# Attention value products in blocks of three key tiles, tied in TensorE's issue order, with the row sums at the head of a block

## Chip, cores and metric

The kernel runs on one core of a Trainium2 chip. The metric is the device time of one execution in microseconds; lower is better.

## What is computed

Two layers of a hybrid backbone over 512 latent tokens with 256 context tokens, model width 1024, all in float32. Layer 0 mixes tokens by multi-head latent attention, layer 1 by a Hyena convolution, and each layer has a gated ConvFFN. The change is in the attention of layer 0: 16 heads, 512 queries, 768 keys (256 of context, 512 latent), head width 96 for scores and 64 for values.

```python
def block_attention(q, k, v):
    def one_block(qblk):
        s = jnp.einsum('bqhd,bkhd->bhqk', qblk, k).astype(F32) * scale
        p = jax.nn.softmax(s, axis=-1).astype(v.dtype)
        return jnp.einsum('bhqk,bkhd->bqhd', p, v)
    o = lax.map(one_block, qb)
    return o.transpose(1, 0, 2, 3, 4).reshape(B, Lq, H * v.shape[-1])

x = x + g1 * (ox @ mla_w_o[j])
```

## The kernel before

Weights and activations are split into a high part rounded to the format fp32r and a low remainder, and a product is three matmuls (high x high, high x low, low x high; `mm3`, L136 to L139). Only the value products and the row sums are in plain float32, each one matmul in the program and two on the chip, as the counts in the trace show.

The attention loop (`attention`, L646, its loop at L842) goes over eight pairs of heads p, in a pair over six key tiles kt of 128 keys, in a tile over the two heads b. For each it does:

- `s_step` (L731): three matmuls give the scores of 128 keys by 512 queries in a PSUM tile `s`; ACT's exponential (L740) writes them to `pf`; GpSimd (POOL) adds `pf` to the head's running sum `acc` (L750; DVE in the last two heads' last tiles). The scores' 97th row carries the negative row maximum of each query, so that the exponential stays in range.
- `side` (L818): work for the next pair n = p + 1, one step a call: rope rows by DMA (`put_rope`), the key products `pk` (`prod_k`, L635), the query products `pq` (`prod_q`, L704), the split of the next query weight where n is odd (`load_wq`: ACT cast L129, DVE subtraction L130), then eight `max_step` (L712): two matmuls into a PSUM tile `sm` of one buffer, and DVE's maximum over it (L721, `mx`). `max_row` (L723) turns four such columns into a row by four small matmuls `mr`, and ACT copies it into the queries (L727). At the end of even pairs it makes the rope part of two more pairs (`prod_rope`, L673: products `pq`, rotation `rot`, DVE steps).
- `v_step` (L754): the value products. The two heads of a pair write the two halves of a PSUM tile `po`, 64 columns of the array each: column tiling. A call takes two key tiles, four products, every second tile, one step behind the scores.
- `row_sums` (L768): a matmul of ones (32 columns wide) with `acc` for each head gives the sums, ACT copies 64 rows of them (L775), two DMAs write them to DRAM, one reads them back as 16 x 64 (L779), DVE takes the reciprocal (L780), and two DMAs broadcast it to 128 partitions (`rb`, L784).
- `normalize` (L787): DVE multiplies the pair's output `ou` by `rb`, ACT casts it to `oh`, DVE subtracts for `ol`.

PSUM tiles of `pst` (scores, key and query products, `mr`, row sums, `rot`) share four buffers. The order on each engine's queue is fixed when the program is built: a scheduler takes the instructions, their dependencies and free buffers, and lists them for each engine; at run time each engine goes through its list in order. So the program's order of calls is only a wish, and value products of one call may be issued apart.

Of the kernel before, what the change touches and what calls it, by code (L numbers as in the profile page):

```python
# [8 lines left out]
F32 = mybir.dt.float32  # L9
# [8 lines left out]
P = 128  # L18
D = 1024
NC = D // P  # L20
T = 512
# [36 lines left out]
def hybrid_kernel(ctx, tc, A, out):  # L58
    nc = tc.nc
    dma = nc.sync.dma_start  # L60
# [1 line left out]
    stt = nc.vector.scalar_tensor_tensor  # L62
    vtt = nc.vector.tensor_tensor
    vts = nc.vector.tensor_scalar
    mm = nc.tensor.matmul

    gp = ctx.enter_context(tc.tile_pool(name="gp", bufs=1, side="right"))
    wp = ctx.enter_context(tc.tile_pool(name="wp", bufs=2, side="right"))
# [4 lines left out]
    def in_order(prev, cur):  # L73
        if prev is not None:
            info = mybir.DependencyInfo(mybir.DependencyClass.NoSync, mybir.DependencyReason.DATA)
            tc.add_manual_dep(cur.ins, prev.ins.name, info, reason="issue order")
        return cur

    def pst(name):
        return psum[0].tile([P, 512], F32, tag="ps", name=name, bufs=psum[1])  # L80

    def pso(name):
        return psum[0].tile([P, 512], F32, tag="o", name=name, bufs=2)
# [22 lines left out]
    ones = gp.tile([P, P], F32, name="ones")  # L106
# [125 lines left out]
    class Norm:  # L232
# [18 lines left out]
        def add(self, xj, h=None):  # L251
            self.n_add += 1
            self.flush(self.nh)
            n, w = self.n, self.nth * P
            hs = list(range(self.nh)) if h is None else [h]
            j = self.j[hs[0]]
            for i in hs:
                self.j[i] += 1
            if j == 0 and n > 2:
                self.acc = self.tmp.tile([P, self.nt * P], F32, tag="sqa", name="sqa", bufs=1)  # L260
                act(out=self.acc, in_=xj, func=AF.Square)
                return
            sq = self.tmp.tile([P, self.nt * P], F32, tag="sq", name="sq", bufs=2)[:, :w * len(hs)]
            if j < n - 1 and n > 2:
                act(out=sq, in_=xj, func=AF.Square)  # L265
                acc = self.acc[:, hs[0] * w:hs[-1] * w + w]
                nc.gpsimd.tensor_tensor(out=acc, in0=acc, in1=sq, op=ALU.add)  # L267
                if j == n - 2:
                    for i in hs:
                        self.due.append((self.n_add, self.acc[:, i * w:(i + 1) * w], i, True, False))  # L270
                return
            vtt(out=sq, in0=xj, in1=xj, op=ALU.mult)
            for i, q in enumerate(hs):
                self.due.append((self.n_add, sq[:, i * w:(i + 1) * w], q, j == 0, j == n - 1))
# [191 lines left out]
    rst = [[dr.tile([2, T], F32, name=f"rst{a}{p}") for p in range(HEADS // 2)] for a in range(2)]  # L466

    def mla():
# [56 lines left out]
        with ExitStack() as st:  # L525
            ab = st.enter_context(tc.tile_pool(name="ab", bufs=1, side="left", reuse_waits="tile"))
            psum_pool(st, "pb", 4)
            return attention(ab, L)
# [117 lines left out]
    def attention(ab, L):  # L646
        at, cosq, sinq, cqh, cql = (L[n] for n in ("at", "cos", "sin", "cqh", "cql"))
# [12 lines left out]
        vf = {}  # L660
# [68 lines left out]
        pts, accs = {}, {}  # L729

        def s_step(h, kt):  # L731
            kh, kl = kb[h % 4]
            qh, ql = qb[h % 4]
            ks = slice(kt * P, kt * P + P)
            s = pst("s")
            mm(s, lhsT=kh[0:97, ks], rhs=qh[0:97], start=True, stop=False)
            mm(s, lhsT=kh[0:96, ks], rhs=ql[0:96], start=False, stop=False)
            mm(s, lhsT=kl[0:96, ks], rhs=qh[0:96], start=False, stop=True)  # L738
            pf = ab.tile([P, T], F32, tag="pf", name="pf", bufs=8)
            act(out=pf, in_=s, func=AF.Exp, scale=ATT_SCALE)  # L740
            pts[h, kt] = pf
            if kt == 0:
                return
            if kt == 1:
                accs[h] = ab.tile([P, T], F32, tag="acc", name="acc", bufs=4)
                prev = pts[h, 0]
            else:
                prev = accs[h]
            add = vtt if h >= HEADS - 2 and kt > 3 else nc.gpsimd.tensor_tensor
            add(out=accs[h], in0=prev, in1=pf, op=ALU.add)  # L750

        pos = {}

        def v_step(p, kts):  # L754
            if kts[0] == 0:
                pos[p] = pso("po")
            for kt in kts:
                for b in range(2):
                    mm(pos[p][64 * b:64 * b + 64], lhsT=vf[p][:, kt, b, :], rhs=pts.pop((2 * p + b, kt)),
                       start=kt == 0, stop=kt == 5)  # L760
            if kts[-1] == 5:
                ou = ab.tile([P, T], F32, tag="ou", name="ou", bufs=2)
                nc.scalar.copy(out=ou, in_=pos.pop(p))
                ends.append((p, ou))

        ends, norm = [], []

        def row_sums():  # L768
            while ends:
                p, ou = ends.pop(0)  # L770
                rsum = pst("rsum")
                for b in range(2):
                    mm(rsum[32 * b:32 * b + 32], lhsT=ones[:, 0:32], rhs=accs.pop(2 * p + b), start=True, stop=True)
                sm = at.tile([P, T], F32, tag="wv", name="sm", bufs=4)
                nc.scalar.copy(out=sm[0:64], in_=rsum[0:64])  # L775
                for b in range(2):
                    dma(out=rst[0][p][b:b + 1, :], in_=sm[32 * b:32 * b + 1])
                rs = ab.tile([16, 64], F32, tag="rs", name="rs", bufs=1)
                dma(out=rs, in_=rst[0][p].rearrange("b (a c) -> (b a) c", c=64))  # L779
                nc.vector.reciprocal(out=rs, in_=rs)  # L780
                dma(out=rst[1][p].rearrange("b (a c) -> (b a) c", c=64), in_=rs)
                rb = ab.tile([P, T], F32, tag="rb", name="rb", bufs=1)
                for b in range(2):
                    dma(out=rb[64 * b:64 * b + 64], in_=rst[1][p][b].partition_broadcast(64))  # L784
                norm.append((p, ou, rb))

        def normalize():  # L787
            while norm:
                p, ou, rb = norm.pop(0)
                vtt(out=ou, in0=ou, in1=rb, op=ALU.mult)  # L790
                nc.scalar.copy(out=oh[:, p, :], in_=ou)
                vtt(out=ol[:, p, :], in0=ou, in1=oh[:, p, :], op=ALU.subtract)

        NP = HEADS // 2
# [4 lines left out]
        for h in range(2):  # L799
            m2 = ab.tile([P, 4, 2], F32, tag="m2", name="m2", bufs=2)  # L800
            mxs[h] = ab.tile([P, 4], F32R, tag="mx", name="mx", bufs=2)
            for qt in range(4):
                for i in range(2):
                    b1 = pst("b1")[:, :384]
                    mm(b1, lhsT=qb[h][0][0:96, qt * P:(qt + 1) * P], rhs=kb[h][0][0:96, i * 384:(i + 1) * 384],
                       start=True, stop=True)
# [11 lines left out]
        def side(n, i):  # L818
            if i == 11 and n % 2 and n + 1 < NP:
                prod_rope((n + 1) // 2)  # L820
            if n >= NP:
                return
            if i == 0:
                put_rope(n)
                if n > 1:
                    prod_k(n, 0, kb, L)
            elif i == 1 and n > 1:
                prod_k(n, 1, kb, L)
            elif i == 2:
                if n > 1:  # L830
                    prod_q(n)
                if n % 2 and n // 2 + 1 < 4:
                    load_wq(n // 2 + 1)
            elif 2 < i < 11:
                max_step(2 * n + (i - 3) // 4, (i - 3) % 4)
                if i == 6 or i == 10:
                    max_row(2 * n + (i == 10))
                if i == 9 and n + 1 < NP:
                    load_v(n + 1)

        pend = []
        for p in range(NP):  # L842
            for kt in range(6):
                for b in range(2):
                    s_step(2 * p + b, kt)
                    side(p + 1, 2 * kt + b)
                if kt % 2 == 0 and pend:
                    v_step(*pend.pop(0))
                if kt == 1:
                    row_sums()  # L850
                if kt == 4:
                    normalize()
                if kt % 2:
                    pend.append((p, (kt - 1, kt)))
        v_step(*pend.pop(0))
        row_sums()
        normalize()
        return oh, ol

# [412 lines left out]
```

## Time and profile before

| | us |
|---|---|
| median of 3 runs | 1474.65 |
| lowest, highest | 1473.51, 1474.66 |
| profiled execution, time | 1473.2 |
| profiled execution, span | 1471.4 |

| engine | busy us | share of the span |
|---|---|---|
| PE (TensorE matmuls) | 1412.3 | 96% |
| PEld (weight loads) | 1086.9 | 74% |
| DVE (VectorE) | 952.1 | 65% |
| ACT (ScalarE) | 556.6 | 38% |
| POOL (GpSimd) | 223.6 | 15% |

The span runs from the first to the last instruction; the time also has what lies around it. A busy time is a sum over records, and matmuls overlap at their ends, so the cost of a matmul in a queue is read from its start to the next start. In a row of the timeline the first number is the start, the second the time from the first start to the last end, and the brackets give an idle time ahead of it and what ended it. Names of tiles follow the program: `po<-pf,vf` is a value product, `rsum<-acc,ones` a row sum, `sm<-kh,qh` a row-maximum product, `mx<-sm` its reduction, `s<-...` a score product, `pj<-...` the output projection behind the loop.

### The profile page before, as it was taken

The numbers are of one execution on the slowest core, as the hardware profiler recorded it, in microseconds if no ns is written. First come the engines' busy times: TensorE is split into PE (matmuls) and PEld (weight loads), VectorE is DVE, ScalarE is ACT, GpSimd is POOL, SyncE is SP. The second block draws the span as 40 slices with busy tenths as digits, with TensorE's granted clock in tenths as the row PEclk, the third lists the DMA queues.
The fourth block names the chain that finished last, engine by engine and source line by source line (L and its number), as shares of the span: only waits on it lengthen the run. The fifth ranks groups of instructions, "written<-read, shape, count | busy, mean of one in ns | idle before, by whom it ended". The sixth has DMA issues, their size and how long they took to land. (4 is left out here: it accounts for less than half of the span.)

```text
span 1471.4 us, 17226 instructions
## 1 busy us (share of the span) xinstructions
PE 1412.3 (96%) x6702; PEld 1086.9 (74%) x6702; DVE 952.1 (65%) x1423; ACT 556.6 (38%) x845; POOL 223.6 (15%) x188
## 2 busy tenths in 40 slices
PE   6899899999998999999999999999899999999997
PEld 3577655555478878787887887887798888888886
DVE  5875655555458877657774589889776553355545
ACT  5444444445423543214432352333234432243420
POOL 4401044343511000000000103321310000000011
PEclk9999999999999999999999999999999999999998
DMA  9672411111363564674522352222323213332121
GB/s 376 210 275 90 136 41 47 33 54 44 123 208 122 174 217 149 222 282 158 185 99 102 129 178 94 87 86 87 114 87 115 78 59 107 115 105 87 59 79 58
DMA packets 46668, 186.56 MB, mean 127 GB/s; under 512 B 5320, under 2 KB 17864, under 8 KB 32380
## 3 DMA queue, kind: packets, MB, share of 16 engines
q1 hardware_dynamic: 46588, 185.48, 36.4%
q8 instruction: 52, 0.85, 0.2%
q14 instruction: 28, 0.23, 0.0%
HBM read 171.29 MB, written 11.60 MB: 124 GB/s over the span
## 5 line engine op out<-in xcount | busy, mean ns | idle before, releaser
L129 ACT CAST wh<-wr 128x1024 fp32r<-128x1024 f32 (+2 forms) x209 | 195.1, 954 | 190.3 <-PE dn L138 89.0
L130 DVE TENSOR_TENSOR wl<-wr,wh 128x1024 fp32r<-128x1024 f32 (+2 forms) x209 | 247.4, 1199 | 30.0 <-ACT wh L129 27.4
L267 POOL TENSOR_TENSOR sqa<-sqa,sq 128x512 f32<-128x512 f32 (+1 forms) x42 | 55.7, 1326 | 845.2 <-ACT sq L265 844.4
L139 PE MATMUL dn<-gh,wl 128*128 128x512 f32 (+1 forms) x396 | 146.8, 371 | 0.0
L137 PE MATMUL dn<-gh,wh 128*128 128x512 f32 (+1 forms) x396 | 146.7, 372 | 0.0
L138 PE MATMUL dn<-gl,wh 128*128 128x512 f32 (+1 forms) x396 | 146.3, 369 | 0.0
L318 DVE SCALAR_TENSOR_TENSOR z<-ua,vec,z 128x511 f32<-128x511 f32 x44 | 33.0, 749 | 111.0 <-ACT z L317 110.9
L931 DVE SCALAR_TENSOR_TENSOR x<-dn,modc,x 128x512 f32<-128x512 f32 (+1 forms) x36 | 24.9, 690 | 109.4 <-PE dn L139 109.4
L317 ACT ACTIVATE z<-ua,vec 128x512 f32<-128x512 f32 x44 | 34.3, 779 | 150.2 <-PE ua L139 150.1
L721 DVE TENSOR_REDUCE mx<-sm 128x1 fp32r<-128x768 f32 x56 | 53.6, 956 | 55.1 <-PE sm L719 54.7
L740 ACT ACTIVATE pf<-s 128x512 f32<-128x512 f32 x96 | 56.8, 597 | 79.9 <-PE s L738 78.4
L137 PEld LDWEIGHTS dn<-gh,wh 128*128 128x128 f32 x396 | 74.4, 188 | 15.6 <-ACT wh L129 0.8
L138 PEld LDWEIGHTS dn<-gl,wh 128*128 128x128 f32 x396 | 74.5, 188 | 14.3
L750 POOL TENSOR_TENSOR acc<-acc,pf 128x512 f32<-128x512 f32 x60 | 77.4, 1306 | 49.6 <-ACT pf L740 48.5
L139 PEld LDWEIGHTS dn<-gh,wl 128*128 128x128 f32 x396 | 74.4, 188 | 13.9
L137 PE MATMUL hz<-hyh,wh 128*128 128x512 f32 (+1 forms) x224 | 81.5, 365 | 0.0
L139 PE MATMUL hz<-hyh,wl 128*128 128x512 f32 (+1 forms) x224 | 81.4, 364 | 0.0
L138 PE MATMUL hz<-hyl,wh 128*128 128x512 f32 (+1 forms) x224 | 81.1, 363 | 0.0
L137 PE MATMUL ua<-hf1h,wh 128*128 128x512 f32 (+1 forms) x192 | 72.5, 378 | 1.1 <-ACT hf1h L307 1.1
L137 PE MATMUL ua<-hf0h,wh 128*128 128x512 f32 (+1 forms) x192 | 73.3, 382 | 0.0
L138 PE MATMUL ua<-hf1l,wh 128*128 128x512 f32 (+1 forms) x192 | 72.6, 378 | 0.5 <-DVE hf1l L308 0.5
L138 PE MATMUL ua<-hf0l,wh 128*128 128x512 f32 (+1 forms) x192 | 73.0, 380 | 0.0
(383 smaller groups left out, 3419.8 us busy)
## 6 DMA issues: line engine op xcount, KB each, us to landing
wr<-in_wup SPq DMA_DIRECT2D x44, 1024.0 KB, 5.1
mw<-in_modw SPq DMA_DIRECT2D x40, 1024.0 KB, 4.8
wr<-in_wdn SPq DMA_DIRECT2D x32, 704.0 KB, 4.2
wr<-in_win SPq DMA_DIRECT2D x12, 1024.0 KB, 5.0
mw<-in_modw SPq DMA_DIRECT2D x16, 512.0 KB, 3.9
fspec<-fs SPq DMA_DIRECT2D x16, 256.0 KB, 3.4
wr<-in_wo SPq DMA_DIRECT2D x4, 1024.0 KB
fq<-fspec SPq DMA_DIRECT2D x8, 512.0 KB
```

Of the source, the lines that this page charges most:

```text
L129: nc.scalar.copy(out=wh[:, c], in_=wr[:, c])
L130: vtt(out=wl[:, c], in0=wr[:, c], in1=wh[:, c], op=ALU.subtract)
L137: mm(ps, lhsT=ah, rhs=bh, start=first, stop=False)
L138: mm(ps, lhsT=ah, rhs=bl, start=False, stop=False)
L139: return mm(ps, lhsT=al, rhs=bh, start=False, stop=last)
L267: nc.gpsimd.tensor_tensor(out=acc, in0=acc, in1=sq, op=ALU.add)
L317: act(out=z, in_=p, func=AF.Identity, bias=b, scale=w1)
L318: stt(out=z[:, 1:T], in0=p[:, 0:T - 1], scalar=w0, in1=z[:, 1:T], op0=ALU.mult, op1=ALU.add)
L721: nc.vector.reduce_max(out=mxs[h][:, qt:qt + 1], in_=b2[:, :, :384], axis=AX.XY)
L740: act(out=pf, in_=s, func=AF.Exp, scale=ATT_SCALE)
L750: add(out=accs[h], in0=prev, in1=pf, op=ALU.add)
L931: i = stt(out=x[:, q, c], in0=job[0][:, c], scalar=mcol(l, 5, q), in1=x[:, q, c], op0=ALU.mult, op1=ALU.add)
```

## The change

`v_step` and `row_sums` become `value_block`. It takes three key tiles of a pair, six products, from the last tile back to the first, and is called for tiles 3 to 5 of the last pair after kt = 0 (block B in the text below) and for tiles 0 to 2 after kt = 3 (block A). From the second pair on, block A has the row sums of the pair before at its head, as matmuls of 64 columns, in the same halves as the value products. The wrapper `mm` records every matmul; a block puts dependencies without a semaphore from all matmuls since the last block to its first one, from each of its own to the next, and from its last one to all that follow. The row sums move from kt = 1 to kt = 3 and `normalize` from kt = 4 to kt = 5. The copy of the sums becomes two copies of one row. `pf` has 11 buffers in place of 8, `acc` moves to the pool `at`, and `sm` has a buffer of its own.

```diff
-    mm = nc.tensor.matmul
+    lane = {"after": None, "since": None}
+
+    def mm(*args, **kw):
+        i = nc.tensor.matmul(*args, **kw)
+        in_order(lane["after"], i)
+        if lane["since"] is not None:
+            lane["since"].append(i)
+        return i
...
-            pf = ab.tile([P, T], F32, tag="pf", name="pf", bufs=8)
+            pf = ab.tile([P, T], F32, tag="pf", name="pf", bufs=11)
...
-                accs[h] = ab.tile([P, T], F32, tag="acc", name="acc", bufs=4)
+                accs[h] = at.tile([P, T], F32, tag="wv", name="acc", bufs=4)
...
+        ous, norm = {}, []
+
+        def value_block(p, kts, sums=None):
+            since, lane["since"] = lane["since"], []
+            if sums is not None:
                 rsum = pst("rsum")
                 for b in range(2):
-                    mm(rsum[32 * b:32 * b + 32], lhsT=ones[:, 0:32], rhs=accs.pop(2 * p + b), start=True, stop=True)
-                sm = at.tile([P, T], F32, tag="wv", name="sm", bufs=4)
-                nc.scalar.copy(out=sm[0:64], in_=rsum[0:64])
+                    mm(rsum[64 * b:64 * b + 64], lhsT=ones[:, 0:64], rhs=accs.pop(2 * sums + b), start=True, stop=True)
+            if kts and kts[0] == 0:
+                pos[p] = pso("po")
+            for n, kt in enumerate(reversed(kts)):
+                for b in (1, 0):
+                    mm(pos[p][64 * b:64 * b + 64], lhsT=vf[p][:, kt, b, :], rhs=pts.pop((2 * p + b, kt)),
+                       start=kts[0] == 0 and n == 0, stop=kts[-1] == 5 and kt == kts[0])
+            block = lane["since"]
+            for i in since:
+                in_order(i, block[0])
+            for i, j in zip(block, block[1:]):
+                in_order(i, j)
+            lane["after"], lane["since"] = block[-1], []
+            if kts and kts[-1] == 5:
+                ous[p] = ab.tile([P, T], F32, tag="ou", name="ou", bufs=2)
+                nc.scalar.copy(out=ous[p], in_=pos.pop(p))
+            if sums is not None:
+                p = sums
+                sm = ab.tile([P, T], F32, tag="sm", name="sm", bufs=1)
                 for b in range(2):
-                    dma(out=rst[0][p][b:b + 1, :], in_=sm[32 * b:32 * b + 1])
+                    nc.scalar.copy(out=sm[64 * b:64 * b + 1], in_=rsum[64 * b:64 * b + 1])
+                    dma(out=rst[0][p][b:b + 1, :], in_=sm[64 * b:64 * b + 1])
...
-                if kt % 2 == 0 and pend:
-                    v_step(*pend.pop(0))
-                if kt == 1:
-                    row_sums()
-                if kt == 4:
+                if kt == 0 and p:
+                    value_block(p - 1, (3, 4, 5))
+                if kt == 3:
+                    value_block(p, (0, 1, 2), p - 1 if p else None)
+                if kt == 5:
                     normalize()
-                if kt % 2:
-                    pend.append((p, (kt - 1, kt)))
-        v_step(*pend.pop(0))
-        row_sums()
+        value_block(NP - 1, (3, 4, 5))
+        value_block(None, (), NP - 1)
+        lane["after"] = lane["since"] = None
         normalize()
```

### The order on the engines, before and after

The first place is PE's list in the second pair (p = 1), from the score product of kt = 1 on; `sm` with `kh_612` and `kh_614` are row-maximum products of the next pair's two heads, `s` with `kh_1342` and `kh_1344` scores of this pair's. Before, behind the query products:

```order
L773 MATMUL rsum<-acc,ones 32x512
L719 MATMUL sm<-kh_612,qh_1346 128x384 x2
L773 MATMUL rsum<-acc,ones 32x512
L736 MATMUL s<-qh_1350,kh_1342 128x512
L737 MATMUL s<-ql_1351,kh_1342 128x512
L738 MATMUL s<-qh_1350,kl_1343 128x512
L736 MATMUL s<-qh_1352,kh_1344 128x512
L737 MATMUL s<-ql_1353,kh_1344 128x512
L719 MATMUL sm<-kh_612,qh_1346 128x384 x2
L738 MATMUL s<-qh_1352,kl_1345 128x512
L759 MATMUL po<-pf,vf 64x512 x3
L719 MATMUL sm<-kh_612,qh_1346 128x384 x2
```

In the changed kernel, from the scores of kt = 3 to block A:

```order
L68 MATMUL s<-qh_1352,kh_1344 128x512
L68 MATMUL s<-ql_1353,kh_1344 128x512
L68 MATMUL s<-qh_1352,kl_1345 128x512
L68 MATMUL sm<-kh_612,qh_1346 128x384 x2
L68 MATMUL mr<-ident_r,mx 1x128
L68 MATMUL sm<-kh_612,qh_1346 128x384 x2
L68 MATMUL mr<-ident_r,mx 1x128 x2
L68 MATMUL sm<-kh_614,qh_1348 128x384 x2
L68 MATMUL rsum<-acc,ones 64x512 x2
L68 MATMUL po<-pf,vf 64x512 x6
```

Row sums and value products, which lay in ones and threes between the `sm` products, now follow all five of them; the last three `sm` ahead of the block have only `mr` between them. Over the whole list 59 groups of column-tiled matmuls become 16: before, 22 of three value products, two of four, 20 of one, one of two, and 14 of row sums; now eight of six and eight of eight.

The second place is DVE's list in the same pass (p = 1), from the query subtractions `ql` of the next pair to the normalization `ou<-ou,rb` of the first pair, whose reciprocal is `rs`. Before:

```order
L633 TENSOR_TENSOR ql_1347<-pq,qh_1346 64x512
L721 TENSOR_REDUCE mx<-sm 128x1
L633 TENSOR_TENSOR ql_1349<-pq,qh_1348 64x512
L721 TENSOR_REDUCE mx<-sm 128x1 x3
L780 RECIPROCAL rs<-rs 16x64
L721 TENSOR_REDUCE mx<-sm 128x1 x3
L790 TENSOR_TENSOR ou<-ou,rb 128x512
L721 TENSOR_REDUCE mx<-sm 128x1
L792 TENSOR_TENSOR ol<-ou,oh 128x512
```

In the changed kernel:

```order
L641 TENSOR_TENSOR ql_1347<-pq,qh_1346 64x512
L729 TENSOR_REDUCE mx<-sm 128x1
L641 TENSOR_TENSOR ql_1349<-pq,qh_1348 64x512
L729 TENSOR_REDUCE mx<-sm 128x1 x6
L793 RECIPROCAL rs<-rs 16x64
L729 TENSOR_REDUCE mx<-sm 128x1
L641 TENSOR_TENSOR kl_1343<-pk,kh_1342 64x384
L641 TENSOR_TENSOR kl_1345<-pk,kh_1344 64x384
L641 TENSOR_TENSOR kl_1343<-pk,kh_1342 64x384
L641 TENSOR_TENSOR kl_1345<-pk,kh_1344 64x384
L803 TENSOR_TENSOR ou<-ou,rb 128x512
L805 TENSOR_TENSOR ol<-ou,oh 128x512
```

The reciprocal goes from behind the fourth reduction of eight to behind the seventh, and the normalization from between the last two reductions to behind the four key subtractions `kl` that follow them.

## Rows read from the trace of the kernel before

**Rows 1.** The page, busy times of the engines (us, share of the span, instructions)
```profile
PE 1412.3 (96%) x6702; PEld 1086.9 (74%) x6702; DVE 952.1 (65%) x1423; ACT 556.6 (38%) x845; POOL 223.6 (15%) x188
```

**Rows 2.** Busy times in the attention loop, by engine; PEclk is the granted clock
```profile
180.00:406.00 226.00, 224.68 (x872) 123.15 (x872) 118.24 (x142) 107.30 (x186) 98.44 (x76) 1.00 0.18 57
```

**Rows 3.** Timeline of PE, end of the loop (start us, us, engine, line, operation)
```profile
391.78 1.05 PE L773 MATMUL rsum<-acc,ones 128*32 128x512 f32 x4
392.76 0.50 PE L736 MATMUL s<-qh,kh 97*128 97x512 f32 x1
...
394.03 0.40 PE L738 MATMUL s<-qh,kl 96*128 96x512 f32 x1
394.36 1.93 PE L759 MATMUL po<-pf,vf 128*64 128x512 f32 x6
396.22 0.50 PE L736 MATMUL s<-qh,kh 97*128 97x512 f32 x1
396.56 0.40 PE L737 MATMUL s<-ql,kh 96*128 96x512 f32 x1
396.79 0.40 PE L738 MATMUL s<-qh,kl 96*128 96x512 f32 x1
...
399.22 1.94 PE L759 MATMUL po<-pf,vf 128*64 128x512 f32 x8
401.08 0.50 PE L736 MATMUL s<-qh,kh 97*128 97x512 f32 x1
```

**Rows 4.** Timeline of PE, a single value product in the second pair
```profile
221.57 1.07 PE L759 MATMUL po<-pf,vf 128*64 128x512 f32 x2
222.58 0.50 PE L736 MATMUL s<-qh,kh 97*128 97x512 f32 x1
```

**Rows 5.** Timeline of PE, row-maximum products and a small matmul
```profile
252.58 0.52 PE L719 MATMUL sm<-kh,qh 96*128 96x384 f32 x2
252.94 0.23 PE L726 MATMUL mr<-ident_r,mx 128*1 128x128 f32 x1
253.00 0.45 PE L737 MATMUL s<-ql,kh 96*128 96x512 f32 x1
```

**Rows 6.** Timeline of PE, first pair, row-maximum products
```profile
183.59 0.52 PE L719 MATMUL sm<-kh,qh 96*128 96x384 f32 x2
...
188.54 0.62 PE L719 MATMUL sm<-kh,qh 96*128 96x384 f32 x2 [0.84 <-DVE mx L721]
```

**Rows 7.** Timeline of DVE, first pair, weight subtraction and reductions
```profile
185.75 1.75 DVE L130 TENSOR_TENSOR wl<-wr,wh 128x512 fp32r<-128x512 f32 x1
187.53 0.96 DVE L721 TENSOR_REDUCE mx<-sm 128x1 fp32r<-128x768 f32 x1
189.20 0.96 DVE L721 TENSOR_REDUCE mx<-sm 128x1 fp32r<-128x768 f32 x1 [0.71 <-PE sm L719]
```

**Rows 8.** Timeline of weight loads, first pair, the same row-maximum product
```profile
188.54 0.30 PEld L719 LDWEIGHTS sm<-kh,qh 96*128 96x128 f32 x2 [1.72 <-DVE mx L721]
```

**Rows 9.** Timeline of ACT, third pair, weight and query casts
```profile
243.09 1.05 ACT L129 CAST wh<-wr 128x1024 fp32r<-128x1024 f32 x1 [1.72 <-PE pq L138]
244.05 0.57 ACT L632 CAST qh<-pq 64x512 fp32r<-64x512 f32 x1
```

**Rows 10.** Timeline of DVE, third pair, first reduction
```profile
247.74 0.94 DVE L721 TENSOR_REDUCE mx<-sm 128x1 fp32r<-128x768 f32 x1
```

**Rows 11.** Timeline of SP's DMA queue, end of the loop
```profile
407.76 0.31 SPq L779 DMA_DIRECT2D rs<-rst  x1
...
412.21 1.09 SPq L784 DMA_DIRECT2D rb<-rst  x2
```

**Rows 12.** Timeline of DVE, end of the loop, reciprocal and normalization
```profile
410.20 0.53 DVE L780 RECIPROCAL rs<-rs 16x64 f32<-16x64 f32 x1
415.72 0.69 DVE L790 TENSOR_TENSOR ou<-ou,rb 128x512 f32<-128x512 f32 x1 [4.98 <-DMA rb<-rst]
```

**Rows 13.** Timeline of ACT, end of the loop, copy of the row sums
```profile
405.67 0.58 ACT L775 COPY sm<-rsum 64x512 f32<-64x512 f32 x1 [0.40 <-PE rsum L773]
```

More of the change, by code (lines that the diff above doesn't have):

```diff
@@ L752, in attention @@
         pos = {}
[L754 to L770, printed above, removed]
+        ous, norm = {}, []
+        def value_block(p, kts, sums=None):
+            since, lane["since"] = lane["since"], []
+            if sums is not None:
                 rsum = pst("rsum")
                 for b in range(2):
-                    mm(rsum[32 * b:32 * b + 32], lhsT=ones[:, 0:32], rhs=accs.pop(2 * p + b), start=True, stop=True)
-                sm = at.tile([P, T], F32, tag="wv", name="sm", bufs=4)
-                nc.scalar.copy(out=sm[0:64], in_=rsum[0:64])
+                    mm(rsum[64 * b:64 * b + 64], lhsT=ones[:, 0:64], rhs=accs.pop(2 * sums + b), start=True, stop=True)
[17 more added lines that the diff above has]
+                sm = ab.tile([P, T], F32, tag="sm", name="sm", bufs=1)
@@ L784, in row_sums @@
                     dma(out=rb[64 * b:64 * b + 64], in_=rst[1][p][b].partition_broadcast(64))
-                norm.append((p, ou, rb))
+                norm.append((p, ous.pop(p), rb))
         def normalize():
@@ L839, in side @@
                     load_v(n + 1)
-        pend = []
+        lane["since"] = []
         for p in range(NP):
```

## Prediction

> **What bounds the kernel now.** I read the page first: TensorE (PE) is busy 96% of the span, VectorE (DVE) 65%, ScalarE (ACT) 38% [rows 1]. [...]
>
> Next, what a column-tiled group (value products, row sums) costs. I read start to start, not busy times, because matmuls overlap in the trace. A lone value product holds PE from 221.57 to 222.58, 1.01 us [rows 4]. A group of three takes 394.36 to 396.22, 1.86, and a group of four 399.22 to 401.08, also 1.86 [rows 3]; the row shows six and eight matmuls because each one is two on the chip. So an odd product costs as much as two: the two column halves work side by side, and a single leaves one half empty. A further pair costs 1.86 - 1.01 = 0.85. Two row sums together take 391.78 to 392.76, 0.98 [rows 3], and a row sum alone leaves its half empty in the same way.
>
> Each group also has edges. A plain score matmul follows the last one by 0.23 (396.56 to 396.79), but the group starts 0.33 after its predecessor (394.03 to 394.36), and the first plain matmul after it holds PE 0.34 (396.22 to 396.56) [rows 3]: 0.10 + 0.11, some 0.20 a group.
>
> **What the change takes off PE.** In the instruction order of before the 96 value products and 16 row sums lie in 59 groups: 24 of three or four products, 21 of one or two, 14 of row sums. 24 x 1.86 + 21 x 1.01 + 14 x 0.98 + 59 x 0.20 = 44.6 + 21.2 + 13.7 + 11.8 = 91.3 us. After it there are 16 groups, eight of six products and eight of six products and two row sums (same tiling, so I cost a row-sum pair as a product pair): 1.01 + 2 x 0.85 = 2.71 and 3.56. 8 x 2.71 + 8 x 3.56 + 16 x 0.20 = 53.4 us. **PE is relieved of 37.9 us**, some 38.
>
> Two things lie in that. A group costs, above its pairs, its edges and 1.01 - 0.85 = 0.16, so the 43 groups that vanish give 43 x 0.36 = 15 us; the other 22 are half-empty pairs.
>
> [...]
>
> **What it puts in its place.** The block is fixed in PE's order: every matmul written before it must be issued before it. Between block B (key tiles 3 to 5) and block A (tiles 0 to 2, with the row sums) stand five of the eight row-maximum steps `sm` of the next pair, and the order shows the last three with nothing but `mr` columns between them. The groups that filled this stretch are gone. An `sm` may start only when DVE has reduced the last one, since the tile has one buffer. When PE waits, a round is 0.66 us from sm to reduce (188.54 to 189.20), 0.96 of reduce and 0.05 back (188.49 to 188.54) [rows 6, 7]: 1.67 us.
>
> Ordinary pair (p = 1, 3, 5, 6). From the first of the five to block A: four rounds and one sm, 4 x 1.67 + 0.36 = 7.04. The work that PE has there: five sm at 0.36 (252.58 to 252.94), four mr columns at 0.06 [rows 5], eleven score matmuls at 0.235, together 4.6. So PE waits 2.4 us. Behind block A three sm follow with two or more score steps between; there I count 0.2 for a round, 0.3 for the last mr (it waits for the last reduce) and 0.35 for the scores that wait for ACT's copy of that mr: 0.85, an estimate from the same rows. Sum 3.3 a pair, **13.2 for four**.
>
> Pairs that also split a weight (p = 2, 4): ACT casts the weight before the query (243.09, then 244.05 to 244.62), and DVE's subtractions push the first reduce to 247.74 [rows 9, 10]. In before the row sums and three value products lay over that. Now the first sm comes 0.6 late and its round takes 247.74 + 0.96 + 0.05 - 244.7 = 4.05 in place of 1.67, 2.4 more. 2.4 + 0.6 + 2.4 + 0.2 (the rope product covers most of the waits behind A) = 5.6, **11.2 for two**.
>
> p = 0: the first sm is at 183.59, the third at 188.54, held by a weight subtraction of 1.75 us ahead of its reduce [rows 6, 7]. Two rounds and one sm more bring block A to 192.2; the work from 183.59 on (five sm, four score steps of 0.7, mr) ends at 188.4. 3.8 of wait, of which 0.84 is there already [rows 6]: **3.0**. p = 7 has no sm: nothing.
>
> Other edits. The row sums' copy becomes two of one row each; by 0.58 a copy [rows 13] that is 4.6 us more on ACT, which stands idle half of the loop: nothing on the path. Their way: copy end 406.25, issue of the read 407.76, reciprocal 410.20, issue of the broadcast 412.21, use 415.72 [rows 11 to 13]. From the start a of block A: sums done a + 1.15, two copies to a + 2.3, reciprocal possible a + 6.3, broadcast used from a + 11.8. The reciprocal stands in DVE's queue ahead of the pair's last reduce, whose sm I put at a + 7.9, so it is in time by 1.6; SP's later transfers sit behind the same chain and are wanted only in the next pair. The normalization comes after DVE's key subtractions or in the middle of the rope steps (about a + 13): in time. Eleven `pf` buffers cover eight tiles in use at a block, and `acc` in another pool follows the same turn. At the end the last chain is longer by one copy, and the projection has work for PE meanwhile.
>
> **Sum.** 37.9 saved, 13.2 + 11.2 + 3.0 = 27.4 of new waits: 10.5 us less. The profiled execution took 1473.2 (span 1471.4), so 1462.7; the median of the runs shown is 1474.65, 1.45 above it. I say **1463**.
>
> Bounds of the waits: below, only the bare rounds, 2.4 in each of seven pairs, 17 us, so 21 less, 1452; above, half as much again, 41, which is 3 slower, 1476. I take 27.4 since its parts are walked from neighbouring rows.
>
> [...]
>
> **Rivals.**
> 1. Few waits: only the bare rounds show, 1452 or less. For it: DVE is idle nearly half of the loop [rows 2]. Against it: a round is a latency, not a load. 0.14.
> 2. No change: waits of 35 to 41 cancel the saving, 1470 to 1476. For it: one more wait of 1.5 us a pair does it, as scores waiting for a PSUM buffer that ACT or DVE frees late. 0.11.
> 3. Slower: the row-sum chain comes late. It starts two key tiles later in the pair than before, and the reciprocal, then the normalization, block DVE's in-order queue ahead of a reduce and of the key subtractions that free PSUM. It has 1.6 us to spare at the reciprocal; beyond that a late microsecond is one on PE in each of seven pairs. At 3.2 us late the gain is gone, at 4.2 the time is 1473 + 7 = 1480. Against it: chain times from rows. 0.10.
> 4. Slower: empty halves are not what costs, and only the edges go: 15 - 27, 12 slower, 1485. Three equal to four, and one to two, in the rows speak against it. 0.03. Small mixes of these, slower too: 0.02.
> That the blocks do not form is excluded by the printed order.
>
> **Numbers.** My forecast, 3 to 20 us faster, has 0.60. Two tenths of a percent, 3 us, is about what a measurement of this kernel can tell from no change. Faster by more: 0.60 + 0.14 = 0.74; within: 0.11; slower: 0.15. For 8 in 10 the range goes from 1449, just under the lower bound of the waits, to 1476, which takes in no change.
>
> **What would show it.** PE, loop: 16 groups, 2.7 and 3.6 us each start to start; if six products take over 3.3, the pairing is wrong. Loop end near 395 instead of 405.5. PE's idle time ahead of sm, released by the reduce, near 15 to 20 us in sum, longest above 2 us at p = 2 and 4. The reciprocal never waiting for its transfer on DVE with PE idle behind it; if it does, rival 3. A loop that ends at 405 or later makes the prediction wrong.

## The result: slower by 0.7%, and the profile after

| | before | after |
|---|---|---|
| median of the runs, us | 1474.66 | 1484.67 |
| lowest, highest | 1473.51, 1474.81 | 1482.94, 1485.03 |
| span of the profiled execution | 1471.4 | 1482.7 |
| ratio, 95% interval | | 1.0067 [1.005, 1.0085] |

The forecast was 1463 and faster; the time lies 9 us above the top of its range, 1476. Of all runs below one, in the experiment with the weight split later, fell out of line, 1709.58 us at a granted clock of 0.75; the 1457.35 given there is the median with it, and 1456.13 is the median of the other three.

The loop ends at the first product of the output projection: 405.53 before, 414.53 after. So 9.0 of the span's 11.3 us have arisen by the loop's end. The timelines of PE, first before, then after:

```profile
405.53 0.50 PE L137 MATMUL pj<-oh,wh 128*128 128x512 f32 x1
```

```profile
414.53 0.50 PE L68 MATMUL pj<-oh,wh 128*128 128x512 f32 x1
```

The busy times of the loop after the change, in the columns of [rows 2]:

```profile
180.00:406.00 226.00, 201.62 (x839) 122.66 (x839) 111.69 (x137) 107.23 (x187) 96.89 (x74) 0.92 0.18 56
```

PE is busy 201.62 us in place of 224.68, so work did leave it. But the granted clock is 0.92 in place of 1.00. The next view has the same columns, in slices of 2 us around block A of pair p = 1:

```profile
218.00:220.00 2.00, 2.00 (x12) 1.46 (x10) 1.79 (x3) 1.59 (x3) 1.98 (x3) 1.00 0.00 0
220.00:222.00 2.00, 1.01 (x6) 0.67 (x6) 0.96 (x1) 0.60 (x1) 2.00 (x2) 1.00 0.00 0
222.00:224.00 2.00, 1.01 (x6) 0.57 (x3) 0.96 (x1) 0.43 (x1) 1.54 (x2) 0.78 0.00 0
224.00:226.00 2.00, 2.00 (x6) 0.53 (x6) 0.96 (x1) 0.16 (x1) 0.00 (x0) 0.50 0.00 0
226.00:228.00 2.00, 2.00 (x10) 0.66 (x8) 0.00 (x0) 1.15 (x2) 0.00 (x0) 0.87 0.00 1
```

From 220 to 224 PE is busy half of the time. Then the granted clock falls to 0.50, and it is back at 1.00 only after 226. What stands in that stretch is shown by PE's timeline:

```profile
220.40 0.22 PE L68 MATMUL mr<-ident_r,mx 128*1 128x128 f32 x1
221.61 0.61 PE L68 MATMUL sm<-kh,qh 96*128 96x384 f32 x2 [0.99 <-DVE mx L729]
222.06 0.22 PE L68 MATMUL mr<-ident_r,mx 128*1 128x128 f32 x1
223.27 0.27 PE L68 MATMUL mr<-ident_r,mx 128*1 128x128 f32 x1 [0.99 <-DVE mx L729]
223.37 0.98 PE L68 MATMUL sm<-kh,qh 96*128 96x384 f32 x2
224.28 1.98 PE L68 MATMUL rsum<-acc,ones 128*64 128x512 f32 x4
226.04 2.99 PE L68 MATMUL po<-pf,vf 128*64 128x512 f32 x12
228.97 0.50 PE L68 MATMUL s<-qh,kh 97*128 97x512 f32 x1
```

Here are the waits of the forecast: PE stands for DVE's reduce, 0.99 us at a time. Behind them the row sums hold PE 224.28 to 226.04, 1.76 us, and the six products 2.93. In pair p = 5 the same block, behind two waits of the same length, ran at clock 1.00:

```profile
352.17 0.62 PE L68 MATMUL sm<-kh,qh 96*128 96x384 f32 x2 [0.99 <-DVE mx L729]
...
353.84 0.22 PE L68 MATMUL mr<-ident_r,mx 128*1 128x128 f32 x1 [0.99 <-DVE mx L729]
...
354.46 1.08 PE L68 MATMUL rsum<-acc,ones 128*64 128x512 f32 x4
355.37 2.74 PE L68 MATMUL po<-pf,vf 128*64 128x512 f32 x12
358.05 0.50 PE L68 MATMUL s<-qh,kh 97*128 97x512 f32 x1
```

0.91 for the sums, 2.68 for the products: that is the price of the forecast. So a stall costs its own length, and in six of the eight pairs part of block A behind it, or all of it, also ran at a granted clock of 0.50. Block A took 4.14 us at p = 0 in place of 2.72, and 4.69, 5.71, 6.31, 5.02 and 5.24 at p = 1, 2, 3, 4 and 6 in place of 3.59; every block B ran at clock 1.00. The longest is that of p = 3:

```profile
289.29 1.98 PE L68 MATMUL rsum<-acc,ones 128*64 128x512 f32 x4
291.06 4.61 PE L68 MATMUL po<-pf,vf 128*64 128x512 f32 x12
```

Which pair is hit I can't read from its waits: from the pair's first `sm` (216.63 and 347.19) to the end of the second wait the rows of p = 1 and p = 5 lie 130.56 or 130.57 us apart, one by one, and only one of the two fell. What decides it is not shown.

**An account of the loop.** From here on every run is told by three numbers of its profiled execution, taken from 180 us to the start of `pj`. Idle is that length less PE's busy time. Lost is the sum, over slices of 1 us, of busy time x (1 - granted clock). Work is busy time less lost, an estimate of what PE would take at clock 1.00: the row sums that held PE 0.91 there held it 1.76 at clock 0.50.

| us | loop | work | idle | lost |
|---|---|---|---|---|
| before | 225.5 | 224.2 | 1.3 | 0.0 |
| after | 234.5 | 193.4 | 25.1 | 16.0 |

225.5 - 30.8 + 23.8 + 16.0 = 234.5. Without the last term the change would have won 7 us in the loop. One caution: 180 us is not quite the same point of the program in every profile. The loop's first score product starts at 180.74 before, at 180.94 after, and between 180.68 and 184.65 in the runs below, so that up to 3.7 us of a run's loop and work lie ahead of its first score product; where that matters it is said. The waits, engine and line waited for (total us, times, longest), first before, then after:

```profile
PE sm L719 <- DVE mx L721: 0.8, 1, 0.8
PE mr L726 <- DVE mx L721: 0.5, 1, 0.5
```

```profile
PE sm L68 <- DVE mx L729: 14.0, 11, 2.5
PE mr L68 <- DVE mx L729: 7.4, 8, 1.1
PE rot L68 <- ACT rph L640: 2.0, 3, 0.7
```

Three theories follow: **theory 1**, the lost clock is a cost beside the waits; **theory 2**, the waits alone make the kernel slower and the clock falls where PE has nothing to do; **theory 3**, the row sums' late chain, or one of the small edits.

### The profile page after: what moved, and what is told of

It is laid out like the page before. It is cut to its first block, busy times and chain, and to the rows that moved or that the text cites. A ratio compares the mean times of both kernels' runs of the same rounds, so it can differ in the third digit from the quotient of the medians.

```text
span 1482.7 us, 17175 instructions
## 1 busy us (share of the span) xinstructions
PE 1400.7 (94%) x6702; PEld 1093.5 (74%) x6702; DVE 948.3 (64%) x1423; ACT 560.5 (38%) x853; POOL 226.3 (15%) x188
```

## Experiments

**Fillers in the waits.** Nothing is taken away; PE only gets spare matmuls to do.

```diff
+            if fill["t"] is not None:
+                for _ in range(4):
+                    last = in_order(last, mm(fill["t"][:, 0:128], lhsT=ones, rhs=ident, start=True, stop=True))
...
+                if i == 5:
+                    fill["t"] = pso("fill")
+                if i == 8:
+                    fill["t"] = None
```

> The changed kernel with four spare matmuls (128x128 f32, results never read, some 0.2 us each by the 0.85 of a 512-column product) behind each of the third to fifth row-maximum products of a pair, where TensorE otherwise waits for the reduce: 84 in all, some 18 us, nearly all of it inside waits. They take no wait away; they only keep TensorE busy in it. Theory 1 (the lost clock is the cause: the stalls let the granted clock fall to 0.50 and the block behind them runs at half speed): the granted clock of the stretch 180 to 406 us rises from 0.92 to 0.98 or more, the value block behind the stalls takes 2.8 us everywhere, the loop ends some 10 us sooner (near 403 in place of 414.5), the time is near 1473. Theory 2 (the waits themselves are the cause, the clock falls only where TensorE has nothing to do): 1484 to 1488, no gain. Theory 3 (late chain of the row sums or another edit): 1484 or more as well.

Measured 1478.43, ratio to before 1.0027 [1.0015, 1.004]; the profiled execution is the fastest of six, 1475.51. Its loop is 230.0 = work 211.9, idle 13.1, lost 5.1. PE in pair p = 1:

```profile
219.02 0.57 PE L68 MATMUL sm<-kh,qh 96*128 96x384 f32 x2
219.43 1.05 PE L68 MATMUL fill<-cst,ones 128*128 128x128 f32 x8
220.24 0.30 PE L68 MATMUL mr<-ident_r,mx 128*1 128x128 f32 x1
...
222.84 1.05 PE L68 MATMUL fill<-cst,ones 128*128 128x128 f32 x8
223.82 1.08 PE L68 MATMUL rsum<-acc,ones 128*64 128x512 f32 x4
224.73 2.75 PE L68 MATMUL po<-pf,vf 128*64 128x512 f32 x12
227.40 0.50 PE L68 MATMUL s<-qh,kh 97*128 97x512 f32 x1
```

The kernel does 18.5 us more work for nothing and ends its loop 4.5 us sooner: 18.5 - 12.0 of idle - 10.9 of lost clock. The sums take 0.91 again. Theory 2 can't give that, since by it work that is put into the waits gains nothing. The gain is some half of what I expected: 6.5 us of fillers stuck out of the waits, and 5.1 us of clock are still lost, around the longest waits at p = 2, 4 and 6.

**The small edits alone**, on the kernel before: eleven `pf`, `acc` in the other pool, row sums as `ones[:, 0:64]`, two copies of one row; the calls stand as before.

```diff
-            pf = ab.tile([P, T], F32, tag="pf", name="pf", bufs=8)
+            pf = ab.tile([P, T], F32, tag="pf", name="pf", bufs=11)
...
-                accs[h] = ab.tile([P, T], F32, tag="acc", name="acc", bufs=4)
+                accs[h] = at.tile([P, T], F32, tag="wv", name="acc", bufs=4)
...
-                nc.scalar.copy(out=sm[0:64], in_=rsum[0:64])
+                    nc.scalar.copy(out=sm[64 * b:64 * b + 1], in_=rsum[64 * b:64 * b + 1])
```

> The kernel before with the edits of the change that are not the order: eleven pf buffers, accumulators in the other pool, row sums as two 64-column products, their copy as two single rows into a buffer of its own. Value products stay where they were. Theories 1 and 2 (all of the loss comes from the order of the value products): within 2 us of the kernel before, 1473 to 1477. Theory 3 (the row sums' chain or the buffers cost): 3 to 10 us above the kernel before.

Measured 1474.82, 0.9996 [0.9985, 1.0006]; loop 226.5 (224.9 from the first score product, before 224.8), idle 1.3, lost 0.0. So none of the loss comes from these edits, and what is left of the change is its order.

**Row-maximum products not tied.** `sm` and `mr` go past the wrapper:

```diff
-                mm(b2[:, i, :384], lhsT=qh[0:96, qt * P:(qt + 1) * P], rhs=kh[0:96, i * 384:(i + 1) * 384],
+                nc.tensor.matmul(b2[:, i, :384], lhsT=qh[0:96, qt * P:(qt + 1) * P], rhs=kh[0:96, i * 384:(i + 1) * 384],
...
-                mm(mr[0:1, qt * P:(qt + 1) * P], lhsT=mxs[h][:, qt:qt + 1], rhs=ident_r, start=True, stop=True)
+                nc.tensor.matmul(mr[0:1, qt * P:(qt + 1) * P], lhsT=mxs[h][:, qt:qt + 1], rhs=ident_r, start=True, stop=True)
```

> The changed kernel, but the row-maximum products and the small transposes are left out of the tie, so that two of the five rounds that stood ahead of the block of tiles 0 to 2 now fall inside it. The value products stay in blocks otherwise. Theory 1 (lost clock): with two waits of 1 us fewer in seven pairs the stalls are short, the clock stays at 0.98 or more in the loop, 14 us of waits and most of the 15 us of lost clock are gone less 3 us for split groups: loop end 395 to 400, time 1462 to 1470. Theory 2 (waits only): 11 us better, near 1473. Theory 3: no better than 1482.

Measured 1465.4, 0.9941 [0.992, 0.9962]; the profiled execution is the slowest of the four, 1470.3. Its loop is 221.8 = work 205.3, idle 9.8, lost 6.8. PE in pair p = 1:

```profile
220.54 1.08 PE L68 MATMUL rsum<-acc,ones 128*64 128x512 f32 x4
221.46 1.02 PE L68 MATMUL po<-pf,vf 128*64 128x512 f32 x2
222.41 0.61 PE L727 MATMUL sm<-kh,qh 96*128 96x384 f32 x2
222.86 0.23 PE L734 MATMUL mr<-ident_r,mx 128*1 128x128 f32 x1
223.01 1.93 PE L68 MATMUL po<-pf,vf 128*64 128x512 f32 x6
224.87 0.22 PE L734 MATMUL mr<-ident_r,mx 128*1 128x128 f32 x1
224.93 0.57 PE L727 MATMUL sm<-kh,qh 96*128 96x384 f32 x2
```

The block is the work that the rounds need: each reduce now runs under value products, and no wait stands between. Splitting the block costs work (a lone product holds PE 0.95, 221.46 to 222.41). Work is 11.9 us above the changed kernel's, of which 3.7 lie ahead of the first score product; yet idle falls by 15.3 and lost by 9.2.

**One bank a tile.**

```diff
-            b2 = psum[0].tile([P, 2, 512], F32, tag="b2", name="sm", bufs=1)
+            for i in range(2):
+                b2 = psum[0].tile([P, 512], F32, tag="b2", name="sm", bufs=2)
...
+                nc.vector.reduce_max(out=m2s[h][:, qt, i:i + 1], in_=b2[:, :384], axis=AX.X)
+            if qt == 3:
+                vtt(out=mxs[h], in0=m2s[h][:, :, 0], in1=m2s[h][:, :, 1], op=ALU.max)
```

> The changed kernel with the row-maximum tile of two PSUM banks and one buffer made into two tiles of one bank each, reduced one by one (0.5 us each by the first pair's reductions) and joined by one small maximum per head: while DVE reads one, TensorE fills the other. A round of 1.67 us becomes 1.1 to 1.2. Theory 1 (lost clock): waits ahead of the block fall from some 3 us a pair to under 1.5, the clock stays near 1.00, loop end 395 to 400, time 1463 to 1470. Theory 2 (waits only): 1.5 to 2 us better in seven pairs, 1470 to 1474. Theory 3: no better than 1482.

Measured 1505.31, 1.0206 [1.0172, 1.024]: theories 1 and 2 are off by 30 us and more, and theory 3's "no better than 1482" names no reason for it. The four runs lie between 1501 and 1510, and the profile is of the slowest, 1510.24. Its loop is 260.0 = work 199.6, idle 27.1, lost 33.3. The waits ahead of `sm` did get shorter, 0.4 us each in place of 1.3, but the small transposes now wait for the maximum that joins the two halves as well:

```profile
PE mr L68 <- DVE mx L733: 13.5, 13, 1.7
PE sm L68 <- DVE m L731: 8.6, 20, 1.7
```

Idle is 2.0 us above the changed kernel's and lost clock 17.3 above it, so the clock is not a mere shadow of the idle time. The slices around one block (columns as above):

```profile
224.00:226.00 2.00, 1.67 (x6) 0.71 (x4) 1.90 (x5) 1.05 (x2) 2.00 (x2) 1.00 0.00 0
226.00:228.00 2.00, 1.59 (x4) 0.60 (x4) 1.84 (x6) 0.00 (x0) 1.57 (x2) 1.00 0.00 0
228.00:230.00 2.00, 1.78 (x7) 1.17 (x7) 0.54 (x3) 0.58 (x1) 0.00 (x0) 0.57 0.00 0
230.00:232.00 2.00, 2.00 (x7) 0.67 (x8) 0.00 (x0) 0.60 (x1) 1.05 (x1) 0.58 0.00 0
```

Ahead of the fall PE counts as busy 80%, but that is four to six matmuls in 2 us, where a full slice has ten to twelve: a pair of these products counts as 0.9 us while it alternates with the reduces, where a pair in a full queue holds PE 0.36 [rows 5]. So idle in a profile understates how little PE does, and the 199.6 of work is too high. Why the smaller rounds lost so much more clock than the changed kernel's is not shown beyond that.

**Blocks of two key tiles, all tied.**

```diff
-                    value_block(p - 1, (3, 4, 5))
-                if kt == 3:
-                    value_block(p, (0, 1, 2), p - 1 if p else None)
-                if kt == 5:
+                    value_block(p - 1, (4, 5))
+                if kt == 2:
+                    value_block(p, (0, 1), p - 1 if p else None)
+                if kt == 4:
+                    value_block(p, (2, 3))
                     normalize()
-        value_block(NP - 1, (3, 4, 5))
+        value_block(NP - 1, (4, 5))
```

> The changed kernel with tied blocks of two key tiles in place of three: tiles 4 and 5 of the last pair behind key tile 0, the row sums and tiles 0 and 1 behind key tile 2, tiles 2 and 3 behind key tile 4. From the account of the loop so far (the changed kernel: 193.4 us of work at full clock, 25.1 idle, 16.0 lost to the clock): eight more blocks at 0.36 each make 3 us more work; no more than two rounds stand back to back ahead of a block, so idle falls to about 10. Theory 1 (lost clock): the loss falls with it to 3 to 6, loop of 209 to 214 us in place of 234.5, time 1461 to 1466. Theory 2 (waits only, clock loss stays as it is): 1469 to 1473.

Measured 1481.61, 1.0033 [1.0021, 1.0046]; loop 234.7 = work 198.4, idle 28.6, lost 7.7; 2.0 of the 5.0 us more work lie ahead of the first score product. The loss fell by half, to a little above the 3 to 6 expected; the idle time did not fall. PE, then DVE, in pair p = 1:

```profile
222.97 0.62 PE L68 MATMUL sm<-kh,qh 96*128 96x384 f32 x2 [1.09 <-DVE mx L729]
223.52 1.08 PE L68 MATMUL rsum<-acc,ones 128*64 128x512 f32 x4
...
232.11 0.62 PE L68 MATMUL sm<-kh,qh 96*128 96x384 f32 x2 [1.05 <-DVE mx L729]
232.66 1.94 PE L68 MATMUL po<-pf,vf 128*64 128x512 f32 x8
```

```profile
227.60 0.96 DVE L729 TENSOR_REDUCE mx<-sm 128x1 fp32r<-128x768 f32 x1 [3.02 <-PE sm L68]
```

I had put the wait down to the number of rounds between blocks. These rows put it down to the tie: ahead of each block PE waits for a reduce, and behind it DVE has stood idle for 3.02 us. The run with blocks of two and `sm` not tied, below, bears that out.

**Row sums early**, as a tied pair of their own, and, in another kernel, **row sums of 32 columns** at the block's head:

```diff
+                if kt == 1 and p:
+                    value_block(None, (), p - 1)
                 if kt == 3:
-                    value_block(p, (0, 1, 2), p - 1 if p else None)
-                if kt == 5:
+                    value_block(p, (0, 1, 2))
+                if kt == 4:
                     normalize()
```

```diff
-                    mm(rsum[64 * b:64 * b + 64], lhsT=ones[:, 0:64], rhs=accs.pop(2 * sums + b), start=True, stop=True)
+                    mm(rsum[32 * b:32 * b + 32], lhsT=ones[:, 0:32], rhs=accs.pop(2 * sums + b), start=True, stop=True)
```

> The changed kernel with the row sums taken from the head of the block and put, as a tied pair of their own, behind key tile 1 (as before the change), and the normalization one key tile sooner. Theory 1: the rounds ahead of the block stay, so do waits and clock loss; eight groups more at 0.3 to 0.4: 1484 to 1488. Theory 3 (the row sums' late chain is the cause): 1481 or less.

> The changed kernel with the row sums as two 32-column products at the head of the block, as before the change, so that the tiling differs from that of the value products behind them. If the same tiling matters, every block with row sums takes an edge more, 0.1 to 0.3 us in eight pairs, 1 to 2.5 us in all on top of 1484; if not, within 1 us of the changed kernel.

Early sums: 1479.44, 1.0028 [1.0014, 1.0043], which is theory 3's number and not theory 1's. The loop does not bear out theory 3's mechanism: idle is 25.1, as in the changed kernel, so taking the chain forward saved no waiting. From its first score product the loop is 2.1 us shorter (231.5 against 233.6), as lost falls by 6.1, to 9.9, against 4.1 us more work. The rest lies behind the loop, where no edit is: from `pj` to the end of the span it is 1065.0 us here and 1068.2 in the changed kernel, and 1063.7 to 1068.9 over all profiles. I take theory 3 as not supported; what moves the stretches ahead of the loop and behind it by these few us stays open. 32 columns: 1485.59, 1.0059 [1.0041, 1.0077], work 194.1 against 193.4. The same tiling is worth under 1 us.

**The weight split later.** In the run with `sm` untied the longest waits left, 2.07 us each, were at p = 2 and 4, behind the weight split of [rows 9, 10]. On top of that run, dependencies without a semaphore put the weight's casts behind the query's and the two subtractions behind the third and the fourth reduce:

```diff
+            for c, m in ((slice(0, 1024), 0), (slice(1024, 1536), 1)):
+                in_order(mark["q"], nc.scalar.copy(out=w[0][:, c], in_=wr[:, c]))
+                in_order(mark[m], vtt(out=w[1][:, c], in0=wr[:, c], in1=w[0][:, c], op=ALU.subtract))
...
+                if i == 6 and n % 2 and n // 2 + 1 < 4:
+                    load_wq(n // 2 + 1)
```

> The kernel with the row-maximum products left out of the tie (1465.4), and the split of the next query weight put behind them: ACT's casts of the weight behind the casts of the query, DVE's two subtractions behind the third and the fourth row-maximum reduce, where TensorE has the block to do. In the run without this the loop had 9.8 us idle and 6.8 lost to the clock, most of both at these weights in the pairs p = 2 and 4. Theory 1 (lost clock): idle 4 to 6, loss 1 to 3, loop 211 to 214 in place of 221.8, time 1455 to 1459. Theory 2 (waits only): 4 to 5 us better, 1461. A wait that only moves behind: 1465.

Measured 1457.35, 0.9864 [0.9835, 0.9893]; loop 210.5 = work 197.8, idle 7.6, lost 5.1. The time is theory 1's, but in part by luck. From the first score product the loop falls by 8.4 us (217.1 to 208.8); idle falls by only 2.2 and lost by 1.7, and the other 4.5 are work, which no theory had in it. Part of that work is in the blocks A of p = 2 and 4: without the later split their row sums lay apart, and their matmuls held PE for 8.38 and 6.62 us, in part at clock 0.50; here both blocks take 4.74. Two controls have the same edit on the kernel before, and on the changed kernel with everything tied:

> Control: the kernel before with nothing but the later split of the query weight (as in the run that came to 1457.35). Its loop has 1.3 us idle and nothing lost to the clock, so by both theories there is nothing to gain: 1472 to 1477. If the place of the split were worth the gain by itself: 1465 or less.

> The changed kernel, all matmuls tied as in it, with nothing but the later split of the query weight. The two longest waits of the loop (pairs p = 2 and 4) go, those of the ordinary pairs stay. Theory 1 (lost clock): idle 25.1 to 19 or 20, loss 16.0 to 9 to 12, loop 222 to 226 in place of 234.5, time 1472 to 1477, so about the kernel before. Theory 2 (waits only): 1479. If two row-maximum products inside the block do not matter and the weights alone do: 1460.

On before: 1474.96, 1.0001 [0.9992, 1.001]. On the changed kernel: 1484.33, 1.0066 [1.0051, 1.0081], no gain where I had expected some 10 us; loop 238.0, idle 25.1, lost 19.1. With `sm` tied, the moved subtraction only holds the next round ahead of the block; DVE, then PE, at p = 2:

```profile
254.05 2.11 DVE L670 TENSOR_TENSOR wl<-wr,wh 128x1024 fp32r<-128x1024 f32 x1
256.08 0.94 DVE L737 TENSOR_REDUCE mx<-sm 128x1 fp32r<-128x768 f32 x1
```

```profile
257.07 0.26 PE L68 MATMUL mr<-ident_r,mx 128*1 128x128 f32 x1 [2.21 <-DVE mx L737]
```

So the later split does nothing by itself, while `sm` untied pays without it (1465.4); the split pays only where the block can lie over it.

**Two-tile blocks with `sm` untied and the weight later**, and **the last waits** on three-tile blocks: early split in the first pair, and block B of p = 6 between the first two score steps of the last pair. The edits of the second:

```diff
+                in_order(mark["q"] if g > 1 else None, nc.scalar.copy(out=w[0][:, c], in_=wr[:, c]))
+                in_order(mark[m] if g > 1 else None, vtt(out=w[1][:, c], in0=wr[:, c], in1=w[0][:, c], op=ALU.subtract))
...
+                    if kt == b == 0 and p == NP - 1:
+                        value_block(p - 1, (3, 4, 5))
-                if kt == 0 and p:
+                if kt == 0 and 0 < p < NP - 1:
```

> As the run that came to 1457.35 (row-maximum products not tied, weight split later), but with blocks of two key tiles in place of three. With the row-maximum products free to fall inside a block, a block no longer puts a wait ahead of itself, so two-tile blocks should cost only their edges, 8 x 0.36 us: loop 210 to 215, time 1456 to 1462. If tied blocks of two are slow for another reason (1481.6 when everything was tied): above 1470.

> As the run that came to 1457.35, with two edits where its loop still waits: in the first pair the weight is split early, as before the change (there its late split held a reduce for 4.24 us and TensorE for 2.25), and in front of the last pair the block of tiles 3 to 5 stands between the first two score steps, over the wait for the last row maximum (0.99 and 0.68 us, and a block at half clock behind them, 4.18 in place of 2.8). Theory 1 (lost clock): 3 us of waits and 2 to 4 of lost clock go: 1451 to 1455. Theory 2 (waits only): 1454 to 1456. No gain: 1457.

Two tiles: 1464.75, 0.9934 [0.9919, 0.9949]; the loop, 214.9, is as expected (idle 6.8, lost 3.2), with 7 us more work than three tiles; the time is 3 above my range, with 1068.9 us behind the loop, the longest of all. The last waits: **1453.37, 0.9856 [0.9839, 0.9872]**, the fastest version. Its loop is 203.9 = work 199.8, idle 4.0, lost 0.0. The time lies in theory 1's range and 0.6 us below theory 2's, too near to tell them apart; the filler run does that. The whole loop, and its end:

```profile
180.00:384.00 204.00, 199.95 (x874) 122.35 (x873) 115.08 (x142) 110.79 (x192) 100.47 (x76) 1.00 0.20 63
```

```profile
383.86 0.50 PE L68 MATMUL pj<-oh,wh 128*128 128x512 f32 x1
```

The clock is 1.00 throughout, as before the change, with 24 us less work in the loop.

## Why the prediction was wrong, step by step

- **Prices of groups: right.** I read 91.3 us for the groups before, 11.8 of them edges. Start to start, and less one wait of 0.84, the groups in the trace of before sum to 79.4 (91.3 - 11.8 = 79.5). At full clock a block takes 2.72, and 3.59 with sums; I had 2.71 and 3.56. So rival 4, whose 1485 is the time that came, is wrong as a mechanism: its number came by luck.
- **Relief of PE: mis-sized, 30.8 in place of 37.9.** 16 x 2.72 + 8 x 0.91 = 50.8 for the new groups, so 28.6 of it is theirs, near my 29.3 without edges. The 8.6 of edges gave only some 2. Two things work against them. An `sm` that starts behind a wait holds PE 0.45 (221.61 to 222.06), not 0.36; over the 11 waits ahead of an `sm` that is 1.0. And the matmul ahead of a wait is counted to its end, an `mr` 0.22 (220.40 to 220.62), where it holds PE 0.06 in a full queue [rows 5]; over 19 waits that is some 3 us, an estimate, of wait that stands under work. The rest I can't place.
- **Waits: right in kind, 23.8 in place of 27.4.** They stand where I put them, ahead of `sm` and `mr`, with 2.07 us at p = 2 and at p = 4. At p = 1, 3 and 5 they are 1.98 in place of 3.3, as those behind block A did not come. One I didn't have: 2.46 at p = 6, where the scheduler put the split of the output projection's weight into this stretch. The weight loads of `sm` waited too, 22.3 us in 23 waits for the reduce.
- **The step that failed: the clock.** I read 1.00 in the loop [rows 2] and priced both sides at it. That 1.00 belonged to a PE that waited 1.3 us in 225, and my own forecast gave it 27 us of waits, most of them just ahead of the blocks. 16.0 us were lost to the clock, 10.2 of them in the blocks themselves (61.0 us start to start, against 50.8). That term turns the forecast's gain of 10.5 us into a loss: with what the other two terms measured, 30.8 and 23.8, the loop would have been 7 us shorter. My upper bound for the waits, 1476, left it out as well, so the range could not hold the result.
- **Rivals.** Few waits, and waits of 35 to 41: both excluded by the 23.8. Rival 3, late chain: no wait for the reciprocal's transfer with PE idle behind it; early sums left the idle time at 25.1. The true case was none of them.

No wait of PE in the changed kernel's loop was above 2.5 us, and the clock fell to 0.50 in six of its eight pairs.

## What to carry to other kernels

A granted clock of 1.00 is a reading of the present order, not a constant: in the loop it was 1.00 before and 0.92 after, and 0.50 behind the waits of six pairs. When a change adds waits to a full TensorE, price the work right behind the waits at that 0.50 too, as one end of the range. Tying matmuls into a block saved what the start-to-start rows promised (28.6 us against 29.3), but it also took the block away from the latency chain that used to run beneath it; leave that chain's matmuls out of the tie, so that the block covers it. Here the round trip between two engines was cured by work to put under it (1465.4 with `sm` not tied, against 1484.67); splitting it into more and smaller trips made it worse (1505.31).

## What the hardware showed that I had not expected

- Behind two waits of 0.99 us ahead of a block the granted clock was 0.50 at p = 1 and 1.00 at p = 5.
- With idle time of 25.1 and 27.1 us, two kernels lost 16.0 and 33.3 us to the clock: busy time in the trace is not the same as matmuls issued (1.59 us of 2 with four matmuls, against 2.00 with ten to twelve).
- A weight subtraction of the same form (128x1024) took 1.20 to 1.23 us where POOL was idle (loops of the kernel before, of the changed kernel and of the run with the weight split later), and 1.41 to 2.11 where POOL added throughout (changed kernel, and the same with the split later). In the first pair of the run with the weight split later it took 4.24, with POOL adding for 3.16 of them. Half the form (128x512) took 0.68 with POOL idle in that run, and 1.77 with POOL adding throughout in the changed kernel. No run changed POOL alone, so the cause is not shown, nor why the first pair is the worst. DVE of that run (weight split later):

```profile
189.37 4.24 DVE L670 TENSOR_TENSOR wl<-wr,wh 128x1024 fp32r<-128x1024 f32 x1
...
347.16 1.23 DVE L138 TENSOR_TENSOR wl<-wr,wh 128x1024 fp32r<-128x1024 f32 x1 [0.39 <-ACT wh L137]
```
